# One copy of a PSUM half moved from ScalarE to VectorE, and the residual loads moved to GpSimd's DMA queue

## The chip, the core and the metric

The kernel runs on one core of a Trainium2 chip. The metric is the device time of one execution in microseconds (us), lower being better. Engine names in the profile: PE is TensorE (PEld its weight loads), DVE is VectorE, ACT is ScalarE, POOL is GpSimd, SP is SyncE, which here does nothing but issue DMAs.

## The reference

One step of a two-layer decoder over 576 tokens (512 of a prompt, 64 new ones), width 2048. Per layer, with rmsnorm(x, g) = x * rsqrt(mean(x^2) + eps) * g:

```
mix  = concat(pooling branch, retention branch) @ w_out
x    = x + rmsnorm(mix, post_g)
ple  = rmsnorm(p @ w_ple, ple_g)            # p: 256 wide, ple: 2048 wide
gate = sigmoid(x @ w_ple_gate + b_ple_gate)
x    = x + gate * ple
```

The change lies in the last four lines: the embedding product p @ w_ple, and the load of the old x for the residual.

## The kernel before

Activations lie transposed: a tile has 128 channels on the partitions and the 576 tokens along the row, worked on in two halves of 288. Sixteen such tiles make the width of 2048. Each fp32 product is done in three passes on a high and a low part of both operands (`L91` on ScalarE makes the high part, `L92` on VectorE the low one), and the large products go through a Strassen-like scheme, whose sums of weight blocks (`S`, `L246`) stand on VectorE or GpSimd.

After the output projection `out_phase` does the following in each layer:

- It squares the mixed tiles, sums them over the channels on TensorE (`L299`), and computes rM, the reciprocal root, by a chain of twelve small VectorE operations (`L317` to `L323`); TensorE spreads the result over the partitions (`L327`), ScalarE copies it out (`L328`).
- The embedding product: 16 column tiles `ct`, each of two halves. For one half TensorE runs six matmuls (`L137`) into one bank of PSUM; ScalarE squares it out of PSUM (`square`, `L342`) and copies it to a tile `part` (`L792`). When both halves of a column tile are copied, SP stores it (`L793`). After every fourth tile TensorE sums the squares over the channels (`together`, `L304`).
- The residual: for each of the first eight mixed tiles m SP loads the old x (`L804`, 288 KB), VectorE multiplies m by post_g and rM (`L805`) and adds x (`L808`); then the sums are split into high and low parts for the gate product. The other eight follow inside the gate product.
- The gate product begins (`L233` in `plain_unit`, TensorE).

The accumulators are a pool of four PSUM banks under the name `acc`. The embedding product, the gate product and the output projection share it. A matmul into a bank waits until the last reader of what lay there has run. The `x` tiles are a pool of four as well, so a fifth load waits until an earlier tile has been added.

Each engine runs its instructions in one fixed order. That order is made by a scheduler when the kernel is built, from the code and the free buffers; it is not the order of the code, and the embedding product, rM and the residual are interleaved in it.

Of the kernel before, what the change touches and what calls it, by code (L numbers as in the profile page):

```python
# [33 lines left out]
def half(ap, h):  # L34
    return ap[:, h * HN:(h + 1) * HN]
# [3 lines left out]
def decoder_kernel(ctx: ExitStack, tc: tile.TileContext, a, decay8):  # L39
    nc = tc.nc  # L40
# [5 lines left out]
    def buf(tag, shape=(P, NT), dt=F32):  # L46
        return sb.tile(list(shape), dt, tag=tag, name=tag, bufs=BUFS.get(tag, 1))
# [32 lines left out]
    def dram(name, n=KT):  # L80
        return [tc.dram_tile([P, NT], F32, name=f"{name}{i}") for i in range(n)]

    x_dram, m_dram = dram("x"), [dram(f"m{l}") for l in range(L)]
# [17 lines left out]
    def load_weights(src):  # L101
        raw = buf("raw", (P, 16, P))
        nc.sync.dma_start(out=raw, in_=src)
        return raw
# [7 lines left out]
    def split_weights(raw, first, n):  # L112
        parts = [split_part(raw[:, c:c + 4]) for c in range(first, first + n, 4)]
        return [(parts[k // 4][0][:, k % 4], parts[k // 4][1][:, k % 4]) for k in range(n)]
# [15 lines left out]
    def gemm(w, xs, new=acc_tile, by_half=False):  # L130
        acc = [new()[:, :HN] for _ in range(2)]
        n = len(w)
        for hs in ((0,), (1,)) if by_half else ((0, 1),):
            for i, ((wh, wl), (xh, xl)) in enumerate(zip(w, xs)):
                for passno, (u, v) in enumerate(((wh, xh), (wh, xl), (wl, xh))):
                    for h in hs:
                        nc.tensor.matmul(  # L137
                            acc[h], u, v[:, h * HN:(h + 1) * HN],
                            start=(i == 0 and passno == 0), stop=(i == n - 1 and passno == 2),
                        )  # L140
        return acc
# [159 lines left out]
    def together(sums, srcs, start, stop):  # L301
        for i, src in enumerate(srcs):
            for q in range(4):
                mm = nc.tensor.matmul(  # L304
                    sums[32 * q:32 * q + 32], ones, src[:, q * QN:(q + 1) * QN],
                    start=start and i == 0, stop=stop and i == len(srcs) - 1,
                )
                if q == i == 0:
                    after_all(mm, [last_square[0]])
# [29 lines left out]
    def square(out, src):  # L339
        if isinstance(src, list):  # L340
            for h in range(2):
                last_square[0] = nc.scalar.activation(half(out, h), src[h], AF.Square)  # L342
        else:
            nc.scalar.activation(out, src, AF.Square)
# [399 lines left out]
    def out_phase(l, raws, ops_out):  # L744
# [30 lines left out]
        for k in range(2):  # L775
            t = buf("x")
# [6 lines left out]
        for c8 in range(2):  # L783
            raw = load_weights(a["w_ple"][l, :, c8 * 8:(c8 + 1) * 8].rearrange("p c k n -> p (c k) n"))
            w = split_weights(raw, 0, 16)
            for c in range(8):
                ct = c8 * 8 + c
                acc = gemm(w[2 * c:2 * c + 2], pp)
                t, sq = buf("part"), buf(("tmp", "tmp", "tmp", "tmp", "g", "g", "u", "u")[ct % 8])
                square(sq, acc)  # L790
                for i in range(2):
                    nc.scalar.copy(half(t, i), acc[i])  # L792
                nc.sync.dma_start(out=ple_dram[l][ct], in_=t)  # L793
                squares.append(sq)
                if len(squares) == 4:
                    together(sums, squares, ct == 3, ct == KT - 1)
                    squares = []

        def residual(first):
            def xs(k):  # L800
                kt = first + k
                m = mo[kt]
                xr = buf("x")
                nc.sync.dma_start(out=xr, in_=a["x"][:, kt] if l == 0 else x_dram[kt])  # L804
                nc.vector.scalar_tensor_tensor(  # L805
                    out=m, in0=m, scalar=vec["post_g"][:, l, kt:kt + 1], in1=rM, op0=ALU.mult, op1=ALU.mult
                )
                nc.vector.tensor_tensor(out=m, in0=m, in1=xr, op=ALU.add)  # L808
                return m
            return xs  # L810
# [65 lines left out]
        for p in range(8):  # L876
            raw = raws.pop(("gate2", p))
            for c in range(2):
                ct = 2 * p + c
                t = buf("part")  # L880
# [15 lines left out]
    for l in range(L):  # L896
        state = in_first(l, raws, ops)
        ops = in_phase(l, raws, *state)
        ops = out_phase(l, raws, ops)
# [93 lines left out]
```

## Time and profile before

| | |
|---|---|
| median of 3 runs | 2200.15 us (2199.71 to 2204.18) |
| the profiled execution | 2199.76 us, of which 2198.0 us from first to last instruction |
| TensorE busy | 2168.8 us (99%), granted clock 1.00 |
| VectorE busy | 1722.3 us (78%) |
| ScalarE busy | 1058.9 us (48%) |
| GpSimd busy | 87.4 us (4%) |
| embedding product, layer 0 / layer 1 | from 866 to 905 us / from 1957 to 1995 us |

The shares are averages over the whole span. In the 20 us from 880, inside the embedding product of layer 0, TensorE is busy for 18.38 us, VectorE for 16.61 and ScalarE for 17.34.

### The profile page before, as it was taken

To read this page: it belongs to the slowest core of one execution; us is meant where nothing else is said; L and a number is where in the kernel's file an instruction comes from. 1 tells how busy PE (TensorE), PEld (TensorE's weight loads), DVE (VectorE), ACT (ScalarE), POOL (GpSimd) and SP (SyncE) were. 2 spreads that over 40 slices of the span, in tenths; PEclk is the share of its full clock that TensorE was granted. 3 is DMA by queue.
4 is the path that set the end of the run, shared out by engine and by line. 5 is a ranking of instruction groups with operands and counts; after the bars stand their busy time and mean duration, and the time that the engine had idled before them with its cause. 6 is when DMAs were issued, how large, how long until landed. Compare 5 with 4: busy or idle time off the path is not lost.

```text
span 2198.0 us, 42624 instructions
## 1 busy us (share of the span) xinstructions
PE 2168.8 (99%) x16692; PEld 2137.7 (97%) x16692; DVE 1722.3 (78%) x3186; ACT 1058.9 (48%) x2097; POOL 87.4 (4%) x65
## 2 busy tenths in 40 slices
PE   8999999999999999999999999999999999999998
PEld 8999999999899999999999999999999999999998
DVE  8789765767589898887877887666775999988865
ACT  5465433444344555655544554434443445556532
POOL 2000000000001110100020000000000001100000
PEclk9999999999999999999999999999999999999999
DMA  6455455555574433656644444455464743336564
GB/s 225 147 195 167 159 170 153 175 168 174 167 247 148 132 119 119 209 175 201 220 156 150 172 156 155 145 181 164 157 192 146 264 147 120 108 121 234 174 197 153
DMA packets 143337, 371.42 MB, mean 169 GB/s; under 512 B 15008, under 2 KB 53408, under 8 KB 122272
## 3 DMA queue, kind: packets, MB, share of 16 engines
q1 hardware_dynamic: 143136, 368.70, 50.8%
q8 instruction: 131, 2.15, 0.4%
q14 instruction: 70, 0.57, 0.1%
HBM read 277.89 MB, written 90.76 MB: 168 GB/s over the span
## 4 chain that ended last, share of the span: by engine, by line
PE 87%; DMA 6%; DVE 4%; ACT 1%; issue 1%; SPq 0%; POOL 0%; ACTq 0%; DVEq 0%; POOLq 0%
PE acc L137 31%; PE acc L117 13%; PE acc L118 13%; PE acc L119 13%; PE acc L233 4%; PE pb L118 3%; PE pb L117 3%; PE pb L119 3%; DMA x<-ple 3%; DMA out_new_ret_s<-m 1%; PE po L137 1%; DVE wl L92 1%; PE po L378 1%; DMA m<-in_state_ret 1%; DVE x L828 1%
## 5 line engine op out<-in xcount | busy, mean ns | idle before, releaser
L137 PE MATMUL acc<-m,wh 128*128 128x288 f32 x3584 | 650.4, 297 | 0.0
L91 ACT CAST wh<-raw 128x512 fp32r<-128x512 f32 x567 | 350.8, 620 | 539.2 <-PE acc L137 279.1
L118 PE MATMUL acc<-m,wh 128*128 128x288 f32 x1944 | 572.7, 295 | 0.0
L117 PE MATMUL acc<-m,wh 128*128 128x288 f32 x1944 | 570.8, 295 | 0.5 <-ACT m L256 0.5
L119 PE MATMUL acc<-m,wl 128*128 128x288 f32 x1944 | 566.5, 295 | 0.0
L137 PEld LDWEIGHTS acc<-m,wh 128*128 128x128 f32 x3584 | 532.3, 188 | 6.9 <-issue 6.2
L92 DVE TENSOR_TENSOR wl<-raw,wh 128x512 fp32r<-128x512 f32 x567 | 404.0, 713 | 126.2 <-ACT wh L91 120.3
L137 PE MATMUL acc<-m,wl 128*128 128x288 f32 x1792 | 391.8, 296 | 0.0
L117 PEld LDWEIGHTS acc<-m,wh 128*128 128x128 f32 x1944 | 364.4, 188 | 1.4 <-ACT m L256 1.0
L118 PEld LDWEIGHTS acc<-m,wh 128*128 128x128 f32 x1944 | 365.0, 188 | 0.0
L119 PEld LDWEIGHTS acc<-m,wl 128*128 128x128 f32 x1944 | 362.5, 188 | 0.2 <-DVE wl L92 0.2
L91 ACT CAST wh<-S 128x512 fp32r<-128x512 f32 x356 | 220.6, 620 | 239.9 <-PE acc L118 142.5
L137 PEld LDWEIGHTS acc<-m,wl 128*128 128x128 f32 x1792 | 290.3, 188 | 1.4 <-issue 1.4
L92 DVE TENSOR_TENSOR wl<-S,wh 128x512 fp32r<-128x512 f32 x356 | 249.7, 703 | 23.7 <-ACT wh L91 22.2
L246 POOL TENSOR_TENSOR S<-raw 128x512 f32<-128x512 f32 x45 | 69.4, 1541 | 1921.1 <-DMA raw<-in_w_out 746.8
L503 DVE TENSOR_TENSOR part<-acc,part 128x288 f32<-128x288 f32 x192 | 79.1, 451 | 73.8 <-PE acc L137 73.0
L246 DVE TENSOR_TENSOR S<-raw 128x512 f32<-128x512 f32 x133 | 93.3, 702 | 9.0 <-DMA raw<-in_w_in 7.0
L118 PE MATMUL pb<-m,wh 128*128 128x288 f32 x324 | 95.5, 295 | 0.0
L117 PE MATMUL pb<-m,wh 128*128 128x288 f32 x324 | 95.1, 294 | 0.0
L119 PE MATMUL pb<-m,wl 128*128 128x288 f32 x324 | 95.0, 293 | 0.0
L256 ACT COPY d<-acc 128x288 f32<-128x288 f32 x228 | 86.0, 394 | 0.0
L261 DVE TENSOR_TENSOR d<-d,acc 128x288 f32<-128x288 f32 x114 | 51.3, 450 | 40.3 <-PE acc L119 40.0
(266 smaller groups left out, 3279.7 us busy)
## 6 DMA issues: line engine op xcount, KB each, us to landing
raw<-in_w_in SPq DMA_DIRECT2D x95, 1024.0 KB, 5.4
raw<-in_w_out SPq DMA_DIRECT2D x32, 1024.0 KB, 4.9
raw<-in_w_gate SPq DMA_DIRECT2D x32, 1024.0 KB, 5.5
proj<-d SPq DMA_DIRECT2D x96, 288.0 KB, 2.1
part<-proj SPq DMA_DIRECT2D x96, 288.0 KB, 3.1
m<-in_state_ret SPq DMA_DIRECT2D x64, 256.0 KB, 3.1
out_new_ret_s<-m SPq DMA_DIRECT2D x64, 256.0 KB, 5.0
x<-m SPq DMA_DIRECT2D x48, 288.0 KB, 3.7
```

The costliest lines, as they stand in the source:

```text
L91: nc.scalar.copy(hi, src)
L92: return nc.vector.tensor_tensor(out=lo, in0=src, in1=hi.bitcast(F32), op=ALU.subtract)
L117: nc.tensor.matmul(out, wh, xh, start=start, stop=False, **kw)
L118: nc.tensor.matmul(out, wh, xl, start=False, stop=False, **kw)
L119: nc.tensor.matmul(out, wl, xh, start=False, stop=stop, **kw)
L137: nc.tensor.matmul(acc[h], u, v[:, h * HN:(h + 1) * HN], start=(i == 0 and passno == 0), stop=(i == n - 1 and passno == 2),)
L233: nc.tensor.matmul(acc[h], w[:, j], xs[h][passno == 1], start=(i == 0 and j == 0 and passno == 0), stop=(i == 1 and j == 3 and passno == 2),)
L246: eng.tensor_tensor(out=s, in0=x, in1=y, op=op)
L256: ops["tail_act"] = nc.scalar.copy(dst, src)
L261: return nc.vector.tensor_tensor(out=dst, in0=dst, in1=src, op=ALU.add)
L378: mm = nc.tensor.matmul(po_s[32 * r:32 * r + 32, bg], qrep[:, dt, b * 32:b * 32 + 32], s0s[r][:, dt], start=(dt == 0), stop=(dt == 1),)
L503: nc.vector.tensor_tensor(out=half(t, h), in0=acc[h], in1=half(t, h), op=ALU.add)
```

## The change

For the first ten column tiles of the embedding product the second half is copied out of PSUM by VectorE instead of ScalarE (the squares stay on ScalarE). And the sixteen residual loads of each layer are issued by GpSimd instead of SP. The rest of the code is the same. Line numbers below the change move on: in the changed kernel the copies are `L791` (ScalarE, first half), `L793` (VectorE) and `L795` (ScalarE, second half of the last six tiles), the store is `L796`, the load `L807`, the multiplication `L808` and the addition `L811`.

```diff
                 square(sq, acc)
-                for i in range(2):
-                    nc.scalar.copy(half(t, i), acc[i])
+                nc.scalar.copy(half(t, 0), acc[0])
+                if ct < 10:
+                    nc.vector.tensor_copy(half(t, 1), acc[1])
+                else:
+                    nc.scalar.copy(half(t, 1), acc[1])
                 nc.sync.dma_start(out=ple_dram[l][ct], in_=t)
...
                 xr = buf("x")
-                nc.sync.dma_start(out=xr, in_=a["x"][:, kt] if l == 0 else x_dram[kt])
+                nc.gpsimd.dma_start(out=xr, in_=a["x"][:, kt] if l == 0 else x_dram[kt])
```

The scheduler places the new copies among VectorE's other work. First place: VectorE in layer 0, the chain of rM (`L318` to `L323`), as a difference (a minus is the order before, a plus the order now).

```order
+L793 COPY part_11230<-acc_11217 128x288
 L319 TENSOR_SCALAR tmp_11164<-tmp_11164 128x144
+L793 COPY part_11251<-acc_11238 128x288
 L321 SCALAR_TENSOR_TENSOR tmp_11164<-tmp_11164 128x144
 L322 TENSOR_TENSOR tmp_11164<-tmp_11164 128x144
 L323 SCALAR_TENSOR_TENSOR tmp_11164<-tmp_11164 128x144
 L321 SCALAR_TENSOR_TENSOR tmp_11164<-tmp_11164 128x144
+L793 COPY part_11272<-acc_11259 128x288
 L322 TENSOR_TENSOR tmp_11164<-tmp_11164 128x144
 L323 SCALAR_TENSOR_TENSOR tmp_11164<-tmp_11164 128x144
 L321 SCALAR_TENSOR_TENSOR tmp_11164<-tmp_11164 128x144
+L92 TENSOR_TENSOR wl_11427<-raw_11416,wh_11426 128x512
```

Three of the copies (column tiles 0, 1 and 2) and one split of weights, which stood behind the chain, now stand inside it.

Second place: VectorE in layer 0 from the end of the eight multiplications on. Before:

```order
L805 SCALAR_TENSOR_TENSOR m35_9276<-m35_9276,c_post_g_977,long_11146 128x576
L808 TENSOR_TENSOR m28_8882<-m28_8882,x_11636 128x576
L808 TENSOR_TENSOR m30_8982<-m30_8982,x_11646 128x576
L808 TENSOR_TENSOR m32_9116<-m32_9116,x_11656 128x576
L808 TENSOR_TENSOR m34_9275<-m34_9275,x_11666 128x576
L92 TENSOR_TENSOR wl_11431<-raw_11416,wh_11430 128x512
L92 TENSOR_TENSOR wl_11717<-raw_11708,wh_11716 128x512
L92 TENSOR_TENSOR m0_11640<-m28_8882,m0_11640 128x288
L808 TENSOR_TENSOR m29_8883<-m29_8883,x_11676 128x576
```

And now, in two pieces; the additions `L811` of m30, m32 and m34 stand between them:

```order
L808 SCALAR_TENSOR_TENSOR m35_9276<-m35_9276,c_post_g_977,long_11146 128x576
L793 COPY part_11293<-acc_11280 128x288
L811 TENSOR_TENSOR m28_8882<-m28_8882,x_11636 128x576
```

```order
L92 TENSOR_TENSOR wl_11431<-raw_11416,wh_11430 128x512
L793 COPY part_11351<-acc_11338 128x288
L793 COPY part_11372<-acc_11359 128x288
L92 TENSOR_TENSOR m0_11640<-m28_8882,m0_11640 128x288
L92 TENSOR_TENSOR wl_11717<-raw_11708,wh_11716 128x512
L793 COPY part_11393<-acc_11380 128x288
L92 TENSOR_TENSOR m1_11650<-m30_8982,m1_11650 128x288
L92 TENSOR_TENSOR m2_11660<-m32_9116,m2_11660 128x288
L811 TENSOR_TENSOR m29_8883<-m29_8883,x_11676 128x576
L92 TENSOR_TENSOR m3_11670<-m34_9275,m3_11670 128x288
L811 TENSOR_TENSOR m31_8983<-m31_8983,x_11684 128x576
L793 COPY part_11448<-acc_11435 128x288
```

The copy of column tile 3 (`acc_11280`) stands behind all eight multiplications, the copies of tiles 5 to 7 behind four additions, and that of tile 8 (`acc_11435`) behind two more, which read x tiles loaded by GpSimd. TensorE's order changes only around the sums `L304`, each of which moves past one or two halves of the product. The matmuls into `acc_11380` (tile 7) take the bank of `acc_11280`, and those into `acc_11477` (tile 10) the bank of `acc_11435`.

Third place: GpSimd in layer 0, as a difference, from the first residual load to the last; the sums `S` of weights are what it did before.

```order
+L807 DMA x_11676<-in_x 128x576
+L807 DMA x_11684<-in_x 128x576
+L807 DMA x_11692<-in_x 128x576
+L807 DMA x_11700<-in_x 128x576
+L807 DMA x_11923<-in_x 128x576
+L807 DMA x_12074<-in_x 128x576
+L807 DMA x_12218<-in_x 128x576
+L807 DMA x_12362<-in_x 128x576
 L246 TENSOR_TENSOR S_12051<-raw_11834 128x512
+L807 DMA x_12506<-in_x 128x576
 L246 TENSOR_TENSOR S_12161<-raw_11989 128x512
```

Four loads stand earlier among the sums of the output projection; these eight follow one another, and a sum of the gate product's weights stands behind them. On SP the same rows are gone, and two stores of the product (`ple04`, `ple03`) have changed places. Both layers have the same pattern.

## Rows read from the trace of the kernel before

**Rows 1.** The page: busy time of each engine.
```profile
PE 2168.8 (99%) x16692; PEld 2137.7 (97%) x16692; DVE 1722.3 (78%) x3186; ACT 1058.9 (48%) x2097; POOL 87.4 (4%) x65
```

**Rows 2.** Waits of TensorE, whole span: waited for, us, times, longest us.
```profile
PE acc L137 <- ACT part L792: 2.8, 4, 1.0
PE po L304 <- ACT tmp L342: 2.2, 2, 1.1
...
PE acc L119 <- DVE wl L92: 0.8, 2, 0.4
```

**Rows 3.** Timeline of TensorE, layer 0: start, us, [idle before it].
```profile
874.69 0.53 PE L137 MATMUL acc<-d,wh 128*128 128x288 f32 x2 [0.95 <-ACT part L792]
...
879.57 1.14 PE L327 MATMUL po<-tmp,pick 128*128 128x144 f32 x8
881.82 1.19 PE L304 MATMUL po<-tmp,ones 128*32 128x144 f32 x32 [1.10 <-ACT tmp L342]
...
893.10 0.43 PE L137 MATMUL acc<-d,wh 128*128 128x288 f32 x2
...
897.08 0.53 PE L137 MATMUL acc<-d,wh 128*128 128x288 f32 x2 [0.34 <-ACT part L792]
...
901.78 0.53 PE L137 MATMUL acc<-d,wh 128*128 128x288 f32 x2 [0.51 <-ACT part L792]
...
905.39 0.53 PE L233 MATMUL acc<-m,wh 128*128 128x288 f32 x2
```

**Rows 4.** The same, layer 1.
```profile
1984.29 0.43 PE L137 MATMUL acc<-d,wh 128*128 128x288 f32 x2
...
1994.81 0.53 PE L233 MATMUL acc<-m,wh 128*128 128x288 f32 x2
```

**Rows 5.** Timeline of VectorE, layer 0.
```profile
874.03 0.68 DVE L92 TENSOR_TENSOR wl<-raw,wh 128x512 fp32r<-128x512 f32 x1
...
877.91 0.31 DVE L323 SCALAR_TENSOR_TENSOR tmp<-tmp 128x144 f32<-128x144 f32 x1
878.69 0.69 DVE L92 TENSOR_TENSOR wl<-raw,wh 128x512 fp32r<-128x512 f32 x1 [0.48 <-ACT wh L91]
881.18 5.92 DVE L805 SCALAR_TENSOR_TENSOR m<-m,c_post_g,long 128x576 f32<-128x576 f32 x8 [1.79 <-ACT long L328]
887.02 2.76 DVE L808 TENSOR_TENSOR m<-m,x 128x576 f32<-128x576 f32 x4
889.70 1.29 DVE L92 TENSOR_TENSOR wl<-raw,wh 128x512 fp32r<-128x512 f32 x2
890.90 0.45 DVE L92 TENSOR_TENSOR m<-m,m 128x288 fp32r<-128x288 f32 x1
893.56 0.76 DVE L808 TENSOR_TENSOR m<-m,x 128x576 f32<-128x576 f32 x1 [2.21 <-DMA x<-in_x]
```

**Rows 6.** Timeline of VectorE, layer 1.
```profile
1972.37 5.92 DVE L805 SCALAR_TENSOR_TENSOR m<-m,c_post_g,long 128x576 f32<-128x576 f32 x8 [1.80 <-ACT long L328]
...
1982.46 0.75 DVE L808 TENSOR_TENSOR m<-m,x 128x576 f32<-128x576 f32 x1
```

**Rows 7.** Timeline of ScalarE, layer 0.
```profile
880.26 0.89 ACT L328 COPY long<-po 128x288 f32<-128x288 f32 x2
...
901.33 0.70 ACT L792 COPY part<-acc 128x288 f32<-128x288 f32 x2 [0.82 <-DMA ple<-part]
```

**Rows 8.** Lines L503 and L246: ns min/median/max of one.
```profile
L503 DVE TENSOR_TENSOR part<-acc,part x192: 428/449/459, 290.4 to 1781.5; 128x288 f32<-128x288 f32 x192
...
L246 POOL TENSOR_TENSOR S<-raw x45: 1272/1297/3687, 23.3 to 2017.8; 128x512 f32<-128x512 f32 x45
```

**Rows 9.** Line L804's loads landing, 885 to 900 and 1970 to 2010 us.
```profile
DMA to landing us min/median/max: 5.5/6.3/7.6
...
DMA to landing us min/median/max: 2.6/5.0/8.1
```

**Rows 10.** Window: length, busy of PE, PEld, DVE, ACT, POOL, clock, DMA share, GB/s.
```profile
890.00:900.00 10.00, 9.48 (x115) 8.37 (x113) 7.79 (x15) 9.10 (x25) 0.00 (x0) 1.00 0.98 332
```

## The prediction

> **What bounds the kernel.** I read the page first. TensorE is busy for 99% of the span and no other engine for more than 78% [rows 1], so an edit pays only as far as it changes what TensorE waits for. The second view is therefore the list of TensorE's waits. The work that is moved stands behind two of its rows: the next matmul of the embedding product waits for ScalarE's copy, 2.8 us in four places, and the token sums wait for ScalarE's squares, 2.2 us in two places, one in each layer [rows 2]. The third view, TensorE's timeline, says where: in layer 0 at 874.69, 881.82, 897.08 and 901.78 us [rows 3]. So ScalarE does hold up TensorE here, but by 5.0 us in all over the two layers. The last of these waits is not for ScalarE's work: its copy at 901.33 had itself waited 0.82 us for a store of an earlier tile [rows 7]. The fourth view, VectorE's timeline, shows what the copies are moved into: the chain of rM, then eight multiplications and four additions, from 881.18 to 889.70 us without a gap [rows 5]. VectorE's order is fixed, so a copy placed there waits until its turn, and with it the PSUM bank that it should free.
>
> **Prices on VectorE.** Starts that follow one another give them [rows 5]: a multiplication (887.02 - 881.18) / 8 = 0.73 us, an addition (889.70 - 887.02) / 4 = 0.67, a weight split (890.90 - 889.70) / 2 = 0.60. The trace has no copy from PSUM on VectorE. The nearest row is an addition of the same 128x288 tile out of PSUM, 0.45 us [rows 8]; a 576-wide addition is busy for 0.76 at a step of 0.67, so neighbours overlap by about 0.08, and I take 0.37 a copy. It could be as little as 0.26 (0.31, the 144-wide operation [rows 5], taken with a slightly smaller overlap), or the full 0.45 with no overlap.
>
> **The chain of rM.** It ended at 877.91 + 0.31 = 878.22 us. Three copies and one weight split now lie inside: 3 x 0.37 + 0.60 = 1.71, so it ends at 879.93. TensorE began to spread the result at 879.57 [rows 3], with 1.35 us to spare, and now begins at about 880.1, 0.5 later. The copy-out by ScalarE [rows 7] and the multiplications follow: they begin at 881.18 + 0.5 = 881.7 and end 8 x 0.73 later, at 887.5.
>
> **The copies behind the multiplications.** The copy of column tile 3 ends at 887.5 + 0.37 = 887.9. Its bank is wanted by the second half of tile 7. TensorE would be there at about 886.4: from 880.1 it has the spreading (881.82 - 1.10 - 879.57 = 1.15), the first sum (1.2) and five halves of the product, each 0.81 (six of them stand between 874.69 and 879.57 [rows 3]). So it stops for about 1.5 us, which is a new wait, for VectorE. Then VectorE has four additions (2.68, to 890.6), a split (0.60, to 891.2), two copies (0.74), a split of m (0.37, like a copy), a weight split (0.60), and the copy of tile 7 (0.37, to 893.3); two splits of m (0.74), an addition, a split of m, an addition and the copy of tile 8 follow: 0.74 + 0.67 + 0.37 + 0.67 + 0.37 = 2.8, so that copy ends at 896.1. The second half of tile 10 needs the bank of tile 8. Before, it began at 893.10 in layer 0 and 1984.29 in layer 1 [rows 3, 4]. TensorE fills the time up to there only in part (tile 8, the sum, tiles 9 and 10), and stands.
>
> **The loads.** Between those two copies stand two additions that read x. The fifth x tile is asked for when the first addition has run, at 887.9 + 0.75 = 888.7, and is wanted at 893.3 + 0.74 = 894.0: it has 5.3 us. By the loads of before, issued on SP, the landing took 5.5 to 7.6 us there, 6.3 in the middle, and 5.0 in the middle in layer 1 [rows 9]; the DMA engines were at 0.98 of their time [rows 10], and the fifth addition waited 2.21 us for x already [rows 5], while in layer 1 it did not [rows 6]. With the medians, and nothing more for the other queue, the addition is late by 6.3 - 5.3 = 1.0 in layer 0 and by nothing in layer 1. What the issue on GpSimd costs no row shows; from below it is nothing, from above one of GpSimd's sums, 1.27 to 1.30 us as a rule [rows 8], for each load.
>
> **The sum.** The second half of tile 10 begins at 896.1 + 1.0 = 897.1 in layer 0, and in layer 1 (1972.37 - 881.18 = 1091.2 later [rows 5, 6]) at 1987.3. From there to the gate product layer 1 took 1994.81 - 1984.29 = 10.5 us, with no wait for copies [rows 4], and I take 10.5 for both. Layer 0: 897.1 + 10.5 = 907.6, against 905.39, +2.2; it gives back the 0.34 and 0.51 us of waits and the gaps around them, since ScalarE has less to do. Layer 1: 1997.8 against 1994.81, +3.0. SP no longer has a load of x ahead of the weights of the output projection; TensorE lost 0.4 us a layer to a late split there [rows 2], so this gives between 0 and 0.8, and I take 0.3. The copy of tile 9 lies behind that of tile 8 and is needed later. On GpSimd a sum of weights for the gate product stands behind the eight loads and comes about 1 us later; the gate product's first 10 us of matmuls hide it, and if they did not, it would cost that 1 us. The sum is 2.2 + 3.0 - 0.3 = **+4.9 us**. Made against the profiled execution (2199.76 us, span 2198.0) it gives 2204.7; the median of the runs lies 0.4 above that execution, so the forecast is **2205.0 us**. A copy of 0.26 or 0.45 moves the eight copies on the path by -0.9 or +0.6 a layer; landings of 2.6 take 1.0 away, and of 8.1 add 1.8 in layer 0 and 2.8 in layer 1. This case's own range is 2202 to 2209.
>
> **The rivals.** (1) *ScalarE's relief decides.* If the copies of tiles 3 and 8 don't hold a bank that TensorE wants, only what ScalarE gives back is left: at most 2.8 + 2.2 of waits and 0.8 of late splits [rows 2], so 5.8, and the time is 2194.4 to 2195.7. For it speaks that the wait of 1.10 at the first sum [rows 3] follows ScalarE's copy-out of rM [rows 7]; TensorE now has a half of the product to do ahead of that sum. Against it: the bank of tile 3 must be free by 886.4, and VectorE is not through its multiplications before 887 even with none of the chain delayed (887.02 [rows 5]). It decides if TensorE is itself later than 888 for another reason. (2) *The two cancel.* The waits on ScalarE go, and those on VectorE stay at 1 to 2 us a layer because the copies are nearer to 0.26 and x comes early: 2199 to 2203, no measurable change. (3) *GpSimd's queue is late.* With 1.3 us for each issue the fifth x tile comes at 888.7 + 1.3 + 6.3 = 896.3 in layer 0 (+1.3 on the sum) and is late by 1.0 in layer 1; with the longest landing of 8.1 it is 1.8 and 3.1 more. The time is then 2207 to 2212. For it speaks that eight loads follow one another on that queue. Against it: they wait for x tiles to come free in any case.
>
> On rival 3 there is a rule. The Trainium skill, "SBUF — State Buffer", section "A bandwidth-pool intuition that's wrong (but worth ruling out)", says that a transfer issued from GpSimd waits for its descriptors while a VectorE copy holds a port that both share: about 620 ns alone became about 3100 ns beside the copy. Taken as it stands it would put some 2.5 us (an estimate from that page) on a load that meets such a copy, 5 us over two layers, and the sum would be near 2210. Its copies run from SBUF to SBUF, while these read PSUM, and no row here shows a load from GpSimd at all, so it stays part of rival 3.
>
> **How the numbers follow.** Plus or minus 0.2%, 4.4 us (2195.75 to 2204.55), is about what a measurement of this kernel can tell from no change. The likeliest case gets 0.53; it straddles the upper bound, with 0.34 above and 0.19 within. Rival 1 has 0.20, faster; rival 2 0.12, no change; rival 3 0.15, slower. That makes faster 0.20, same 0.31, slower 0.49. The range goes from 2195.5 to 2210.0: it leaves out most of rival 1 and a third of rival 3, about 0.2 together.
>
> **What the profile after would show.** TensorE's waits for `L792` shrink to the first one of each layer, and a row appears in which the product waits for VectorE's copy `L793`, near 888 and 896 us and again 1091 later, some 3 us a layer. The spreading of rM begins 0.5 us later than before. The copies take about 0.37 to 0.45 us. The gate product begins at about 907.6 and 1997.8. If the waits for `L793` are there but short, the step on the copies' price or on VectorE's queue is wrong; if the fifth addition waits for x by more than 1 us, GpSimd's queue is the cause; if the waits for `L792` and for the squares stay, ScalarE was not relieved. The forecast is wrong above all if TensorE reaches tile 7 later than I think, since then the copy of tile 3 is hidden.

## The result and the profile after

| | before | changed kernel |
|---|---|---|
| median | 2199.0 us (6 runs, 2196.56 to 2204.18) | 2217.99 us (6 runs, 2214.66 to 2223.85) |
| ratio | | 1.0084 (95% interval 1.0071 to 1.0097) |
| profiled execution | 2199.76 us | 2223.85 us, span 2222.0 us |

The change costs 19.0 us by the medians. The sign was forecast, the size was not: 4.9 us were expected, and 2218.0 lies above the range. The profiled execution of the changed kernel is the slowest of its six runs. It was already 3.9 us later when it came to the embedding product of layer 0 (its first wait there ends at 878.55 us, against 874.69 [rows 3]), mostly from a wait of 3.25 us for a load of pool state and the half clock that followed it (0.50 from 590 to 594 us); waits for such loads differ from profile to profile. So times inside the embedding product are compared below after that shift. Two executions of the sets below, one of the kernel before with 5466.55 us and one of the last experiment with 12098.47 us, are in the medians but not in the ratios.

The page of the changed kernel, busy time and DMA queues. TensorE is busy 9.5 us longer than before [rows 1] for the same instructions, which points in part at its clock; GpSimd's queue (`software_dynamic`) is new.

```profile
PE 2178.3 (98%) x16692; PEld 2145.9 (97%) x16692; DVE 1731.4 (78%) x3206; ACT 1055.9 (48%) x2077; POOL 103.6 (5%) x97
...
q1 hardware_dynamic: 138528, 359.26, 48.8%
q0 software_dynamic: 2560, 9.44, 1.4%
```

TensorE's waits in the changed kernel (engine, what waits, for whom: us in all, times, longest).

```profile
PE acc L137 <- ACT part L791: 15.3, 6, 7.3
...
PE acc L137 <- DVE part L793: 3.7, 4, 1.6
...
PE po L304 <- ACT tmp L342: 0.6, 2, 0.3
```

Against [rows 2], the waits for squares shrank from 2.2 to 0.6 us, as ScalarE's relief should have it, and the wait for VectorE's copies that was forecast is there with 3.7 us. But the waits for ScalarE's copies, which were to fall, rose from 2.8 to 15.3 us, one of them 7.3 us long. TensorE's timeline in layer 0 shows where; the bracket is the idle time ahead of the row and what ended it.

```profile
878.55 0.53 PE L137 MATMUL acc<-d,wh 128*128 128x288 f32 x2 [0.95 <-ACT part L791]
...
883.86 1.25 PE L327 MATMUL po<-tmp,pick 128*128 128x144 f32 x8 [0.27 <-DVE tmp L323]
...
886.21 1.19 PE L304 MATMUL po<-tmp,ones 128*32 128x144 f32 x32 [0.31 <-ACT tmp L342]
...
890.64 0.54 PE L137 MATMUL acc<-d,wh 128*128 128x288 f32 x2 [0.66 <-ACT part L791]
...
891.92 0.53 PE L137 MATMUL acc<-d,wh 128*128 128x288 f32 x2 [0.22 <-DVE part L793]
...
900.07 0.53 PE L137 MATMUL acc<-d,wh 128*128 128x288 f32 x2 [1.61 <-DVE part L793]
...
905.88 0.85 PE L137 MATMUL acc<-d,wh 128*128 128x288 f32 x2 [4.74 <-ACT part L791]
...
916.88 0.42 PE L233 MATMUL acc<-m,wh 128*128 128x288 f32 x2
```

And in layer 1:

```profile
2000.30 0.53 PE L137 MATMUL acc<-d,wh 128*128 128x288 f32 x2 [1.61 <-DVE part L793]
...
2008.68 0.85 PE L137 MATMUL acc<-d,wh 128*128 128x288 f32 x2 [7.32 <-ACT part L791]
...
2019.56 0.42 PE L233 MATMUL acc<-m,wh 128*128 128x288 f32 x2
```

After the shift the gate product (`L233`) begins 7.6 us later than before in layer 0 (916.88 - 905.39 - 3.86, [rows 3]); from the second half of tile 10 on (900.07, 2000.30) it takes 16.8 and 19.3 us in the two layers, where 10.5 was forecast. Inside these stretches lie the waits of 4.74 and 7.32 us for a copy by ScalarE. ScalarE's timeline says what that copy was waiting for: not for its engine, but for a store of an earlier tile, for 5.07 us.

```profile
894.35 0.40 ACT L791 COPY part<-acc 128x288 f32<-128x288 f32 x1
...
899.68 0.67 ACT L91 CAST m<-m 128x576 fp32r<-128x576 f32 x1 [0.22 <-DVE m L811]
905.42 0.40 ACT L791 COPY part<-acc 128x288 f32<-128x288 f32 x1 [5.07 <-DMA ple<-part]
```

VectorE's timeline, over the same time. Its copies ran where the order had put them, the copy of tile 3 at 891.42 after the multiplications, those of tiles 5 and 6 at 895.06, of tile 7 at 896.76 and of tile 8 at 899.57; that of tile 9 waited for a store as well.

```profile
885.58 5.92 DVE L808 SCALAR_TENSOR_TENSOR m<-m,c_post_g,long 128x576 f32<-128x576 f32 x8 [1.05 <-ACT long L328]
891.42 0.45 DVE L793 COPY part<-acc 128x288 f32<-128x288 f32 x1
891.78 2.76 DVE L811 TENSOR_TENSOR m<-m,x 128x576 f32<-128x576 f32 x4
894.46 0.68 DVE L92 TENSOR_TENSOR wl<-raw,wh 128x512 fp32r<-128x512 f32 x1
895.06 0.81 DVE L793 COPY part<-acc 128x288 f32<-128x288 f32 x2
...
896.76 0.45 DVE L793 COPY part<-acc 128x288 f32<-128x288 f32 x1
...
899.57 0.45 DVE L793 COPY part<-acc 128x288 f32<-128x288 f32 x1
...
905.37 0.46 DVE L793 COPY part<-acc 128x288 f32<-128x288 f32 x1 [2.75 <-DMA ple<-part]
```

SP's DMA issues (start, time from the first to the end of the last issue, count). The first five stores were issued from 879.16 to 892.22 as their tiles were copied. Then nothing until 895.17: the next load of weights, 1 MB, had to wait for the weight split that VectorE ran at 894.46, and right behind it, from 895.60 on, come the stores of tiles 5, 6 and 7.

```profile
879.16 13.06 SPq L796 DMA_DIRECT2D ple<-part  x5
895.17 0.33 SPq L103 DMA_DIRECT2D raw<-in_w_gate  x1
895.60 16.97 SPq L796 DMA_DIRECT2D ple<-part  x8
```

GpSimd's loads of x, 288 KB each, begin at 892.83, when VectorE's first additions free the x tiles:

```profile
892.83 1.87 POOL L807 DMA_DIRECT2D x<-in_x  x3 [40.57 <-DVE m L811]
894.96 0.55 POOL L807 DMA_DIRECT2D x<-in_x  x1 [0.26 <-issue]
```

How long the stores took to land, from the first group (issued from 879 to 892 us) and then the two issued at 895.6 and 896.1:

```profile
DMA to landing us min/median/max: 2.1/2.1/2.3
```

```profile
DMA to landing us min/median/max: 9.8/10.2/10.6
```

Slow landings are not new in this stretch: in the kernel before, the three stores issued from 892 to 898 us landed after 7.0 to 8.9 us. But the stores of tiles 5 to 7 had been issued from 886.4 to 889.7 us there (that of tile 5 5.3 us earlier, after the shift: 895.6 - 886.4 - 3.9), and they landed sooner:

```profile
DMA to landing us min/median/max: 2.1/4.5/6.0
```

The windows of 2 us (length; busy time of PE, PEld, DVE, ACT, POOL; granted clock; DMA share; GB/s) show both sides. Between 890 and 892 the DMA engines moved nothing; between 898 and 906 they were full or nearly so (0.90 to 1.06). And TensorE's clock, granted at 1.00 (2.4 GHz) until TensorE stood idle, fell to 0.50 (1.2 GHz) between 902 and 904, while it stood, and came back between 908 and 910, when it had worked again.

```profile
890.00:892.00 2.00, 1.14 (x7) 0.90 (x7) 2.00 (x5) 1.16 (x4) 0.00 (x0) 1.00 0.00 0
898.00:900.00 2.00, 0.46 (x4) 0.23 (x2) 2.00 (x5) 1.78 (x5) 0.54 (x1) 1.00 1.06 335
900.00:902.00 2.00, 1.06 (x6) 0.83 (x6) 2.00 (x5) 0.36 (x1) 0.54 (x1) 1.00 0.90 230
902.00:904.00 2.00, 0.00 (x0) 0.00 (x0) 0.62 (x1) 0.00 (x0) 0.54 (x1) 0.68 1.03 408
904.00:906.00 2.00, 0.12 (x1) 0.12 (x1) 0.63 (x2) 0.58 (x2) 0.00 (x0) 0.50 1.04 421
906.00:908.00 2.00, 2.00 (x9) 2.00 (x10) 0.49 (x1) 1.44 (x5) 0.54 (x1) 0.50 0.56 221
910.00:912.00 2.00, 2.00 (x40) 1.62 (x38) 1.02 (x2) 2.00 (x7) 0.00 (x0) 1.00 0.98 381
```

So one block of VectorE's work, eight multiplications and four additions from 885.58 to 894.46, held back three things that are DMAs: the stores (their copies stood behind it), the weights (their split did) and the loads of x (the additions free the tiles). They were let go within 4.5 us of one another (892.83 to 897.2): 1 MB of weights, four loads and three stores of 288 KB make 3.1 MB, which at the 350 GB/s that the four windows from 898 to 906 show on average take some 9 us. The stores, issued last, landed after 9.8 to 10.6 us; the copies of tile 9 need a part tile that such a store holds, since there are four; the banks of PSUM stay full, and TensorE stands. Both parts were needed: issued 5.3 us earlier, as before, the store of tile 5 would have landed at 900.1 us even if it had taken 9.8 us, before ScalarE stood ready to copy tile 9 (905.42 - 5.07 = 900.35); and had it landed after 2.1 us, it would have been in time as it was issued (an estimate from these rows).

### The profile page after: what moved, and what is told of

The parts are those of the page before. It is cut to its first block, busy times and chain, and to the rows that moved or that the text cites. A ratio compares the mean times of both kernels' runs of the same rounds, so it can differ in the third digit from the quotient of the medians.

```text
span 2222.0 us, 42669 instructions
## 1 busy us (share of the span) xinstructions
PE 2178.3 (98%) x16692; PEld 2145.9 (97%) x16692; DVE 1731.4 (78%) x3206; ACT 1055.9 (48%) x2077; POOL 103.6 (5%) x97
## 4 chain that ended last, share of the span: by engine, by line
PE 92%; DMA 4%; DVE 3%; issue 1%; ACT 1%; SPq 0%; POOL 0%; ACTq 0%; DVEq 0%; POOLq 0%
PE acc L137 35%; PE acc L117 13%; PE acc L118 13%; PE acc L119 13%; PE acc L233 4%; PE pb L118 3%; PE pb L117 3%; PE pb L119 3%; DMA out_new_ret_s<-m 2%; PE po L137 1%; DMA ple<-part 1%; PE po L378 1%; DMA m<-in_state_ret 1%; PE po L327 1%; DVE wl L92 1%
## 5 line engine op out<-in xcount | busy, mean ns | idle before, releaser
L246 POOL TENSOR_TENSOR S<-raw 128x512 f32<-128x512 f32 x45 | 68.1, 1513 | 1761.5 <-DMA raw<-in_w_out 1336.8
L503 DVE TENSOR_TENSOR part<-acc,part 128x288 f32<-128x288 f32 x192 | 79.1, 451 | 73.8 <-PE acc L137 73.1
L246 DVE TENSOR_TENSOR S<-raw 128x512 f32<-128x512 f32 x133 | 93.4, 702 | 11.0 <-DMA raw<-in_w_in 6.1
```

Source lines behind the costliest of these rows:

```text
L246: eng.tensor_tensor(out=s, in0=x, in1=y, op=op)
L503: nc.vector.tensor_tensor(out=half(t, h), in0=acc[h], in1=half(t, h), op=ALU.add)
```

## The experiments

All ratios are against runs of the kernel before on the same chip; the medians of before in the four sets were 2199.84, 2199.88, 2198.6 and 2201.15 us. "Stage" is the time from the last sum of squares for rM (`L299`) to the gate product in the profiled execution, in layer 0 and layer 1: 32.4 and 30.6 us before, 40.0 and 42.5 in the changed kernel. Theory A: late copies make late stores, and copies wait for those through the part tiles. Theory B: the loads on GpSimd's queue take the DMA engines from the stores. Theory C: the wait is for PSUM banks alone, as the prediction had it.

**Copies on VectorE alone.**

```diff
-                nc.gpsimd.dma_start(out=xr, ...)
+                nc.sync.dma_start(out=xr, ...)
```

> VectorE's copies are kept, the residual loads go back to SP; VectorE's order keeps the copies of tiles 3 and 5 to 8 behind the eight multiplications. Theory A (the copies behind VectorE's residual work make the stores of tiles 5 to 7 late; these are issued among the weight and x loads, land after 8 to 10 us, and copies that need the four part tiles wait for them): still slower than before by 12 to 22 us, with TensorE waiting 4 to 7 us for a first-half copy in each layer. Theory B (the loads on GpSimd's queue take the DMA engines from the stores): the stores land within 6 us and the time is that of the record's sum without its queue, 2202 to 2206.

Measured: 2216.94 us, ratio 1.0081 (1.0066 to 1.0096), stage 39.2 and 39.2 us. TensorE's waits:

```profile
PE acc L137 <- ACT part L791: 9.6, 6, 3.3
...
PE acc L137 <- DVE part L793: 5.0, 4, 2.3
```

The copies alone bring nearly all of the loss, with the residual loads on SP. The longest waits are shorter than expected (3.3 us), but of the same kind: ScalarE's copies waited 7.0 us for stores. Theory B falls as the main cause.

**Loads on GpSimd alone.**

```diff
-                if ct < 10:
+                if ct < 0:
                     nc.vector.tensor_copy(half(t, 1), acc[1])
```

> Only the residual loads are moved to GpSimd; all copies stay on ScalarE. Theory A: the stores are early as before, so the time is within 3 us of before, and TensorE's waits in the embedding product stay near the 2 us a layer of before. Theory B: the loads on GpSimd hold up the stores here too; 5 us or more slower than before, with ScalarE waiting several us for a store.

Measured: 2206.33 us, ratio 1.0028 (1.0016 to 1.0041), stage 31.8 and 33.6 us. Theory A's expectation misses, and theory B's holds for this run: 6 us slower than before, and ScalarE's copies wait 4.9 us for stores. The loads do cost something of their own, though a third of the loss. The profiled execution (2202.87 us) is the second fastest of its eleven, so it shows less than the median lost. In layer 1 TensorE waits 1.61 us for such a copy, which it did not before, and its clock falls to 0.50 right after:

```profile
1990.84 0.53 PE L137 MATMUL acc<-d,wh 128*128 128x288 f32 x2 [1.61 <-ACT part L791]
```

```profile
1992.00:1994.00 2.00, 2.00 (x10) 2.00 (x10) 1.82 (x3) 2.00 (x6) 0.00 (x0) 0.50 0.65 257
```

**Six tiles instead of four for the copies, in the changed kernel.** The two extra tiles have the name `held`.

```diff
-    BUFS = {..., "part": 4, "x": 4, ...}
+    BUFS = {..., "part": 4, "held": 2, "x": 4, ...}
...
-                t, sq = buf("part"), buf(...)
+                t, sq = buf("held" if ct % 3 == 2 else "part"), buf(...)
```

> The changed kernel with six instead of four tiles for the copies (four part, two held). VectorE's copies stay behind its residual work as they were. Theory A: the stores still land after 8 us or more, but the copy that waited for one now has a free tile; the long waits of 4.7 and 7.3 us shrink below 2 us, the clock stays at 1.00, and the time falls by 10 to 16 us against the changed kernel, to the waits for VectorE's copies alone (2202 to 2208). Theory C (the banks alone, as the prediction had it): no change, 2214 to 2222.

Measured: 2208.13 us, ratio 1.0044 (1.0028 to 1.006), stage 35.4 and 36.9 us. The time fell by about half of the loss with the copies as late as in the changed kernel (tile 3's begins 14.6 us after the start of the last `L299` in layer 0 of both), so theory C falls. The size of theory A was missed: stores landed after up to 11.2 us, six tiles did not cover that, and in layer 1 TensorE still waited 3.3 us.

```profile
PE acc L137 <- ACT held L791: 5.0, 2, 3.3
...
PE acc L137 <- ACT part L791: 3.2, 4, 1.0
```

**Only the copies that stand ahead of the multiplications** (tiles 0, 1, 2 and 4), loads on GpSimd.

```diff
-                if ct < 10:
+                if ct in (0, 1, 2, 4):
```

> The changed kernel with VectorE copying only for tiles 0, 1, 2 and 4, whose copies stand inside the chain of rM and ahead of the multiplications; loads on GpSimd. Theory A: no copy is late, so the stores are early, the waits of 4.7 and 7.3 us go, and the time is within 4 us of before. Theory B: the loads are still on GpSimd, so most of the loss stays, 2210 or more.

Measured: 2204.87 us, ratio 1.0027 (1.0015 to 1.0039), stage 33.9 and 32.9 us. Neither expectation is met to the letter (5 us above before; 4 at most and some 10 were expected), but without the late copies 13 of the 19 us are gone. What is left is as much as the loads alone cost.

**The same work in another order on VectorE.** The eight multiplications and additions are held behind given copies on their own engine, so that the copies of tiles 3 and 5 to 9 take their turns among them; nothing else is changed in the code.

```diff
+                    held[ct] = nc.vector.tensor_copy(half(t, 1), acc[1])
...
+                n = min(len(turn), 7)
+                turn.append(k)
+                with tc.issue_after(held[(3, 3, 3, 3, 5, 5, 6, 6)[n]].ins) if first == 0 else ExitStack():
                     nc.vector.scalar_tensor_tensor(...)
+                with tc.issue_after(held[(7, 7, 7, 8, 9, 9, 9, 9)[n]].ins) if first == 0 else ExitStack():
                     nc.vector.tensor_tensor(out=m, in0=m, in1=xr, op=ALU.add)
```

> The changed kernel, same work on the same engines and queues; only VectorE's order is other: the copies of tiles 3 and 5 to 9 stand between the multiplications and additions, each about where its half of the product is ready. Theory A (late copies make late stores): VectorE's copies end by about 881, 885, 887 and 888 us after the layer's start is lined up, the stores of tiles 5 to 7 are issued 7 to 9 us earlier, the waits of 4.7 and 7.3 us for a first-half copy go or fall below 2, the clock stays at 1.00, and the time comes down by 11 us or more, to 2198 to 2207. Theory B (GpSimd's queue): the loads and stores are the same, so most of the loss stays, 2212 or more.

Measured: 2202.31 us, ratio 1.0007 (0.9998 to 1.0016), stage 34.0 and 31.8 us. This is the run that decides: same instructions, engines, queues and tiles, and about 16 us less by the medians, so VectorE's order is the cause. This execution reaches the stage 2.0 us earlier than that of the changed kernel; after that shift the copies of tiles 3, 5 and 7 begin 5.2, 5.0 and 2.4 us earlier (tile 3: 891.42 - 884.18 - 2.0), less than the 7 to 9 us expected of the stores, and it is enough. The stores of tiles 5 to 7 landed after 5.0 to 7.9 us here, so the order makes them both earlier and quicker to land; this run does not tell which of the two counts for more.

```profile
884.18 0.46 DVE L793 COPY part<-acc 128x288 f32<-128x288 f32 x1 [1.67 <-ACT tmp L342]
...
888.07 0.45 DVE L793 COPY part<-acc 128x288 f32<-128x288 f32 x1
...
892.32 0.45 DVE L793 COPY part<-acc 128x288 f32<-128x288 f32 x1
```

In layer 0 TensorE waits for ScalarE's copies in two places, 0.95 us at the first one, as before, and 2.13 us behind a copy that again waits 4.1 us for a store. The clock was not at 1.00 throughout, as expected: it was at 0.50 from 898 to 900 us, right after that wait, and partly so in the windows on either side (0.83 and 0.81).

```profile
897.06 0.64 PE L137 MATMUL acc<-d,wh 128*128 128x288 f32 x2 [2.13 <-ACT part L791]
```

**That order, loads on SP.**

```diff
-                nc.gpsimd.dma_start(out=xr, ...)
+                nc.sync.dma_start(out=xr, ...)
```

> As the kernel with the copies placed in turn, and the residual loads on SP again. Theory A: the loads on GpSimd cost 5 us by themselves (the run with the loads alone was 2206.3 against 2199.8), so this is 3 to 6 us faster than the kernel with the copies in turn and the loads on GpSimd, and within 4 us of before, 2195 to 2203. Theory B': on SP the loads stand among the stores, so it is no faster than that kernel.

Measured: 2206.05 us, ratio 1.002 (1.0009 to 1.003), stage 32.5 and 32.1 us. A miss: it is not faster than with the loads on GpSimd. Copies waited 5.9 us for stores here, against 4.1; its runs spread from 2199.6 to 2208.3 us, and why is not settled. The profile is of one of the fast ones (2200.68 us), so it does not show what the others lost.

**The early copies, loads on SP.** The edit of the early copies and that of the loads together.

> VectorE copies for tiles 0, 1, 2 and 4 alone, residual loads on SP. Against the same copies with the loads on GpSimd (2204.9) theory A expects 3 to 6 us less, so 2198 to 2202, no measurable change from before. If the four copies inside the chain of rM themselves cost 5 us, it stays at 2204 to 2206.

Measured: 2201.6 us, ratio 1.0009 (0.9997 to 1.0022), stage 30.5 and 31.5 us; no change that can be told from before. The four copies, three inside the chain of rM and one right behind it, cost nothing that shows.

**Six tiles in the kernel before.** The edit of the tiles, alone.

> The kernel before with six instead of four tiles for the copies. Its copies waited 2.6 us in all for stores, and TensorE lost 0.34 and 0.51 us to such copies in layer 0: at most 1 us faster by that, so 2197 to 2201. If the four tiles were a hidden bound of before too, 3 us faster or more.

Measured: 2199.68 us, ratio 0.9989 (0.9979 to 0.9998), stage 30.2 and 30.2 us. No copy waits for a store any more, and the two stages are 2.6 us shorter. In the whole time little of that shows: the ratio is the only one here whose interval lies below 1, by about 2 us, but the medians are 0.2 us apart.

**Token sums two column tiles later, with six tiles, all copies on ScalarE.**

```diff
-                if len(squares) == 4:
-                    together(sums, squares, ct == 3, ct == KT - 1)
-                    squares = []
+                if len(squares) == 6:
+                    together(sums, squares[:4], ct == 5, False)
+                    squares = squares[4:]
+        together(sums, squares, False, True)
```

> The kernel before with six tiles for the copies, and each token sum called two column tiles later, so that it no longer follows ScalarE's squares at once. The wait of 1.10 us at the first sum of each layer goes (2.2 us in all) on top of the kernel with six tiles alone (2199.7, ratio 0.9989): 2195 to 2198. If ScalarE is the bound of that stretch whatever the order, the wait only moves to the next matmul and the time stays at 2198 to 2201.

Measured: 2200.96 us, ratio 1.0011 (1.0 to 1.0022). The second reading holds: the wait of 1.10 us at the sum is gone, and one of 1.40 for ScalarE's copy stands in its place.

```profile
880.88 0.54 PE L137 MATMUL acc<-d,wh 128*128 128x288 f32 x2 [1.40 <-ACT part L792]
```

**Loads on GpSimd alone, six tiles.** The edits of the loads alone and of the tiles together.

> Loads alone on GpSimd, copies on ScalarE, six tiles for the copies. If what the loads cost (6.5 us in the run with four tiles) comes by the stores, for which copies wait, it is 3 us or more faster than with four tiles, 2199 to 2203, and the profile shows no copy that waits for a store. If it comes from elsewhere, 2204 to 2208.

Measured: 2199.78 us, ratio 1.0004 (0.9993 to 1.0014), stage 30.2 and 30.2 us. What the loads cost with four tiles (1.0028) is gone with six, and no copy waits for a store. The loads, too, cost time through the stores, as far as can be told.

**Copies in turn, six tiles, loads on GpSimd.**

> The copies placed in turn, loads on GpSimd, six tiles. The wait of 4.1 us of a copy for a store that was left goes, and with it TensorE's wait of 2.1: 1 to 3 us faster than with four tiles (2202.3), 2199 to 2202. If nothing depends on the tiles any more, no change.

Measured: 2197.85 us, ratio 1.0 (0.9989 to 1.001), stage 30.1 and 30.6 us. Both edits of the change are in it, and the loss is gone (the time is below the 2199 expected, on a chip on which the kernel before was 1.3 us faster as well); what remains of the wait for ScalarE's copies is the first one of each layer.

```profile
PE acc L137 <- ACT part L791: 1.9, 2, 1.0
```

**The same, loads on SP.**

> The copies placed in turn, six tiles, and the residual loads on SP. With four tiles this order was 2206.0 with the loads on SP and 2202.3 with the loads on GpSimd; with six tiles and GpSimd it was 2197.9. If the queue of the loads matters only through the stores that copies wait for, it is now 2196 to 2201. If the loads on SP cost something by themselves in this order, 2202 to 2207.

Measured: 2202.93 us, ratio 1.001 (0.9999 to 1.0022), stage 30.3 and 30.3 us. Inconclusive: the time lies in the range of the second reading, but on a chip on which the kernel before took 2201.15 us; the ratio's interval includes 1 and meets that of the run before. The stage is as short as there, so what this execution took more (2204.1 us against 2197.0) lies outside of it.

## Why the prediction was wrong

**What bounds the kernel**: right. The loss is made of TensorE's waits. In the two layers the waits listed in the product were 4.95 us before (2.90 and 2.05) and are 20.1 after (8.8 and 11.3), 15.1 more. Half clock cost most of the rest: from 905.88 TensorE took 3.73 us for 15 matmuls that take 2.0 at full clock, and in layer 1 from 2008.68 3.46 us for 14 that take 1.86, 3.3 us in all. That is 18.4 of the 19.5 us by which the two stages grew.

**The price of a copy**: right. It is busy for 0.45 us, and starts follow 0.36 to 0.37 apart (891.42 and 891.78; 896.76 and 897.13).

```profile
L793 DVE COPY part<-acc x20: 446/450/460, 878.6 to 2008.2; 128x288 f32<-128x288 f32 x20
```

**The chain of rM and the copies behind the multiplications**: right. TensorE begins to spread rM 0.4 us later than before, by [rows 3] and the shift (0.5 forecast). The copy of tile 3 begins at 891.42 (891.4 forecast, with the shift), that of tile 7 ends at 897.1 (897.2), that of tile 8 at 899.9 (900.0 without a wait for x). The second half of tile 10 begins at 900.07, 0.9 us earlier than forecast.

**The wait at tile 7**: too large. 1.5 us were forecast and 0.22 measured, since TensorE had lost 0.31 us at the sum and 0.66 to a ScalarE copy ahead of it, with gaps around both, and came 1.4 us later. It did not matter, since the wait at tile 10 (1.61) sets what follows.

**The loads**: wrong, nothing in place of 1.0 us. The fifth addition never waited for x. The loads took 3.0 to 8.5 us to land, 3.7 in the middle, no slower than SP's 2.6 to 8.1, 4.0 in the middle, over the whole of before. The rule of the Trainium skill that was weighed ("SBUF — State Buffer", "A bandwidth-pool intuition that's wrong (but worth ruling out)") would have put some 2.5 us on a load, by the prediction's estimate; beside these copies, which read PSUM, the landings show no such delay. Another page of the Trainium skill ("VectorE: DVE Perf Modes", "Why PSUM operands drop a tier") says that a PSUM operand keeps a copy out of the mode that needs both ports, and these landings fit that. No run here has a copy of the kind that the first page describes, so neither page is tested.

```profile
L807 POOL DMA_DIRECT2D x<-in_x x16: 538/538/686, 778.5 to 977.1; - x16
...
DMA to landing us min/median/max: 3.0/3.7/8.5
```

**The step that failed** is in the sum: "From there to the gate product layer 1 took 1994.81 - 1984.29 = 10.5 us, with no wait for copies [rows 4], and I take 10.5 for both", and that layer 0 "gives back the 0.34 and 0.51 us of waits". It took 16.8 and 19.3 us. With these in place of 10.5, and the loads' 1.0 taken out, the forecast's own sum would have been 4.9 + 6.3 + 8.8 - 1.0 = 19.0 us, the loss by the medians (that it meets it so exactly is chance: the 16.8 and 19.3 are of one execution, the slowest). The late copies were followed to the PSUM bank and no further; "The copy of tile 9 lies behind that of tile 8 and is needed later" put nothing on the copies that were to wait for stores. But a copy that is late makes its store late, and the store holds one of four part tiles until it lands. The rows that spoke of it were shown: a copy of before had waited 0.82 us for a store [rows 7], and the DMA engines were at 0.98 [rows 10]. I read the first as one more wait that the change would give back, and the second for the loads of x alone. The order alone undoes it (1.0084 to 1.0007), the tiles alone undo half (1.0044), and both together all of it (1.0).

**The rivals**: none of the three had this mechanism. The third looked at DMAs near 895 us, but at the issue and landing of the loads: an issue took 0.54 us on GpSimd, not 1.3, the loads were in time, and it was the stores that came late. Alone the loads cost 1.0028, alone the copies 1.0081, together 1.0084; that these do not add up fits that both make copies wait for the same stores.

**What stays open**: whether, and why, the order with the copies in turn is faster with the loads on GpSimd than on SP (1.0007 and 1.002 with four tiles, 1.0 and 1.001 with six; the intervals of each pair meet). With six tiles the stage takes as long either way, so a difference, if there is one, arises outside of it. Open too is how much of the slow landing of the stores comes from the DMAs let go together.

## What to carry to other kernels

Work that is moved to another engine's queue is late by what stands ahead of it there, and what must be followed is everything that its result releases: the bank that it frees, the store that waits for it, and the tile that this store holds until it lands. Where one block of work on an engine holds back several DMAs at once, they collide when it ends, so count the bytes let go together. Before moving work off an engine that seems full, look at whether its waits are for data or for a tile: here two more tiles ended every wait of a copy for a store and made the two stages 2.6 us shorter, and the moved copies, even placed well, brought nothing that could be measured.

## What the runs showed of the hardware

A DMA issue occupies GpSimd for 0.54 us (538 ns in most of 32 issues), SP for 0.33; the loads themselves landed no later than SP's beside a VectorE that was busy for most of the time. In the changed kernel TensorE's clock fell to 0.50 while TensorE stood idle for 4.7 and 7.3 us, and one matmul then took 0.24 us from start to start instead of 0.13. The length of the stop alone does not tell whether it falls. It also fell to 0.50 after stops of 1.61 us (the loads alone, layer 1) and 2.13 us (the other order, layer 0), when TensorE was already at work again; and it stayed at 1.00 around a stop of 2.11 us (the early copies, layer 0) and one of 3.28 us in the kernel before, for a load of state. The matmul behind that stop and the window that holds its start of work:

```profile
587.71 1.07 PE L378 MATMUL po<-m,u 128*32 128x256 f32 x16 [3.28 <-DMA m<-in_state_ret]
```

```profile
588.00:590.00 2.00, 2.00 (x26) 1.53 (x19) 1.23 (x2) 0.59 (x1) 0.00 (x0) 1.00 0.09 28
```
